# First expert's rows gathered into a slot of the weight ring, and 40 unread identity products, at a handover from mixers to experts

## The chip, the cores and the metric

One core of one Trainium2 chip runs the whole program. The metric is the device time of one execution, in microseconds. The instruction streams are PE (TensorE), DVE (VectorE), ACT (ScalarE), POOL (GpSimd) and SP (SyncE, which here only issues transfers). ACT and POOL issue transfers too.

## The reference

One layer of a hybrid encoder over 1024 tokens of width 1024, in float32:

```
h = x
h = h + hybrid_mixer(rms_norm(h, norm1_g), ...)       # mLSTM heads and gMLP groups, then @ w_out
h = h + hierarchical_moe(rms_norm(h, norm2_g), ...)
return rms_norm(h, final_g)

# hierarchical_moe, for each token: the best of 4 groups, its 2 best of 8 experts
hid = silu(xblk @ w_gate[e]) * (xblk @ w_up[e])        # 1024 -> 512
y[token] += row_w * (hid @ w_down[e])                  # 512 -> 1024
```

There are 32 experts. The weights of one are three matrices of 2 MB each, 192 MB in all.

## The kernel before, in words

The mixer runs over two halves of 512 tokens (`half_mixer`). A product of precision float32 is made of three fast products (`mm3`): each operand is split into a rounded part `r` (ACT, `ACTIVATE wr`) and a rest `l` (DVE, `TENSOR_TENSOR wl`); `split` does it for a chunk of weights, four of which can be split ahead (`SPL`).

At the end of the second half `last_out` makes the last output columns of four token tiles of 128. For each tile it adds the residual, stores it to `hd`, multiplies by norm2's gain (`scaled`, L706), transposes it (`flip`), makes the router's logits (`raw_logits`, `logits_c`), scales the rows by their norm and stores them to `xd` (`normed`, L749). Routing has five parts: `route_a` takes the maxima on DVE, `route_pr` counts the earlier tokens of each expert on PE, `route_so` and `route_c` make the places of the rows and, for the first three experts, whose numbers are fixed, the list of their tokens (`toki`, L873), and `route_d` (L885, twice for each tile) scatters a token's number and weight from POOL into the table `slots` at the places `idxs`. `ranks` then sorts the other 29 experts by their counts, with a last product on `ohp` (L913); the result, `perm`, is read by SP and POOL as the numbers of the experts whose weights and rows come next. Engines' orders inside `last_out` are written out by hand; what follows up to the second expert is ordered by the scheduler, by its own estimate of times. Later experts on PE, DVE and ACT are again in the written order.

The experts go one by one through gate, up and down (`Expert`). `fetch` gathers an expert's rows from `xd` to a tile `xe0`, `xe1` or `xe2` (L1042, an indirect transfer that POOL issues); PE transposes them (`prep`, L1102), ACT and DVE split the transposes into `xer` and `xel` (`split_ps`), and these are the operands of the gate and up products. `following` prepares the next expert's rows during the current one. The three `xe` tiles lie where the mixer's tiles lay (`stA`).

Weights come in chunks of 0.5 MB (`wchunk`), nearly all issued from SP, in the order of use. A chunk goes into the next slot of a cycle of 30: 14 of ring "early", 9 "late", 4 "ring" and 3 "tail", the last being tiles that held the mixer's transposed activations (`slot`). A load can be issued when the slot's last chunk has been split or multiplied. Loads for the first three experts are issued ahead (`prefetch`); five more go to other tiles of the activations (`prefetch_first`). In `last_out` ACT issues three chunks of the third expert's w_down into the three "tail" slots (`held`, `PD`), before the routing of the last tile. Chunks for the experts after that wait for `perm` and a free slot.

Of the kernel before, what the change touches and what calls it, by code (L numbers as in the profile page):

```python
# [15 lines left out]
AF = mybir.ActivationFunctionType  # L16
# [3 lines left out]
P = 128  # L20
T = 1024
# [4 lines left out]
TT = HALF // P  # L26
# [14 lines left out]
       [48] * 4 + [40] * 3 + [64]  # L41
SPL = 4
LOOK = 8
YS = (5, 7)
E_ = mybir.EngineType
TMS = (E_.DVE, E_.Activation)
# [10 lines left out]
TAGS = [n + str(c) for c in (2, 3, 0, 1) for n in "rl"]  # L57
MIX = "TTTSSBSSHSSBSSBSSHSSBSBSBBSBBSSS"
PF = [0, 4, 4, 5]
PD = 3  # L60
ENGS = (mybir.EngineType.SP, mybir.EngineType.Pool)
KO = [4, 5, 6, 7, 0, 1, 2, 3]
MAXX = 48
# [6 lines left out]
def trunk_kernel(ctx: ExitStack, tc: tile.TileContext, x, norm1_g, w_in, conv_qk, b_igate, b_fgate,  # L70
# [264 lines left out]
    def half_mixer(hf):  # L335
# [319 lines left out]
        for nh in range(2):  # L655
            hv = slice(nh * 512, (nh + 1) * 512)
            if last and nh:
                ws = {c: wo(c, nh) for c in CO}
                def piece(po, t, i):
                    part(po, CO[i], ws[CO[i]], t)  # L660

                with tc.manual_schedule(engines=set(MS)):
                    last_out(hf * TT, ys, piece, hv)
                with tc.issue_after(pin["POOL"].ins):
                    route_d(T // P - 2, 0)
                    route_d(T // P - 2, 1)
                    route_d(T // P - 1, 0)
                    route_d(T // P - 1, 1)
                break
            if nh:  # L670
                po = [acc() for _ in range(TT)]
                for c in CO:
                    w = wo(c, nh)
                    for t in range(TT):
                        part(po[t], c, w, t)
            elif last:
                prefetch(XO + RE + RL)
            for t in range(TT):
                nc.vector.tensor_tensor(ys[t][:, hv], po[t], ys[t][:, hv], op=OP.add)
                if last:  # L680
                    nc.sync.dma_start(hd[ds((hf * TT + t) * P, P), hv], ys[t][:, hv])
# [19 lines left out]
    def scaled(g, h, q, eng=None):  # L701
        if q == 0:
            t = g % TT
            xns[g] = yl[0][t - 1] if t else ring.tile([P, 1024], F32, name="raw")
        hv = slice(q * 512, (q + 1) * 512)
        (eng or nc.gpsimd).tensor_tensor(xns[g][:, hv], h[:, hv], g2b[:, hv], op=OP.mult)  # L706
# [26 lines left out]
    def logits(g, h):  # L733
# [4 lines left out]
        for q in range(2):  # L738
# [2 lines left out]
            nc.vector.scalar_tensor_tensor(xn, h[:, hv], rs, g2b[:, hv], op0=OP.mult, op1=OP.mult)  # L741
            nc.gpsimd.dma_start(xd[ds(g * P, P), hv], xn)

    def last_out(g0, ys, piece, hv):
        def normed(t):
            rs = logits_c(g0 + t)
            xn = xns[g0 + t]
            nc.scalar.activation(xn, xn, AF.Copy, scale=rs)
            nc.scalar.dma_start(xd[ds((g0 + t) * P, P)], xn)  # L749

        yl[0] = ys
        flip(g0, ys[0], 0)
        for t in range(TT):
            po = acc()
            piece(po, t, 0)
            if t:
                raw_logits(g0 + t - 1, 1)
                normed(t - 1)
                if t > 1:
                    route_d(g0 + t - 2, 0)  # L760
            piece(po, t, 1)
            piece(po, t, 2)
            if t:
                route_a(g0 + t - 1)
            piece(po, t, 3)
            if t:
                route_pr(g0 + t - 1)
            raw_logits(g0 + t, 0)
            nc.vector.tensor_tensor(ys[t][:, hv], po, ys[t][:, hv], op=OP.add)
            if t:  # L770
                route_so(g0 + t - 1)
            nc.scalar.dma_start(hd[ds((g0 + t) * P, P), hv], ys[t][:, hv])
            flip(g0 + t, ys[t], 1)
            scaled(g0 + t, ys[t], 0)
            if t + 1 < TT:
                if t > 1:
                    route_d(g0 + t - 2, 1)
                scaled(g0 + t, ys[t], 1)
                flip(g0 + t + 1, ys[t + 1], 0)
            if t:  # L780
                route_c(g0 + t - 1)
            if t + 1 == TT:
                prefetch_first()
            prefetch(XO + RE + RL + PF[t])
        scaled(g0 + TT - 1, ys[TT - 1], 1, nc.vector)
        raw_logits(g0 + TT - 1, 1)
        normed(TT - 1)
        prefetch(XO + RE + RL + PF[-1], eng=nc.scalar)
        for z in sources(NSTAT - 1, 2)[:PD]:
            held.append(wchunk(z, nc.scalar, True))  # L790
        route_d(g0 + TT - 3, 1)
        route_a(g0 + TT - 1)
        route_pr(g0 + TT - 1)
        route_so(g0 + TT - 1)
        route_c(g0 + TT - 1)
# [88 lines left out]
    def route_d(t, c):  # L884
        st = nc.gpsimd.indirect_dma_start(  # L885
            out=slots, out_offset=bass.IndirectOffsetOnAxis(ap=idxs[:, t, c:c + 1], axis=0),
            in_=pay[:, t, c], in_offset=None)
        for o in scat:
            tc.declare_no_dep(st.ins, o.ins, reason="every pair has a slot of its own")
        scat.append(st)  # L890
# [7 lines left out]
    def ranks():  # L898
        pc_ = sm()
        for b in range(T // P):  # L900
            nc.tensor.matmul(pc_[:MAXX, :NE], ones[:, :MAXX], masks[:, b], start=b == 0, stop=b == T // P - 1)
        for b in range(T // P):
            nc.tensor.matmul(pc_[:NE, NE:NE + 1], masks[:, b], ones[:, :1], start=b == 0, stop=b == T // P - 1)
        key = lp[0].tile([NE, NE], F32, name="key")
        nc.vector.scalar_tensor_tensor(key, pc_[:NE, :NE], float(NE), keyr, op0=OP.mult, op1=OP.add)
        kc = rt.tile([NE, 1], F32, name="kc")
        nc.vector.scalar_tensor_tensor(kc, pc_[:NE, NE:NE + 1], float(NE), keyc, op0=OP.mult, op1=OP.add)
        rk = rt.tile([NE, 1], F32, name="rk")
        nc.vector.tensor_scalar(key, key, kc, None, op0=OP.is_gt)
        nc.vector.tensor_reduce(rk, key, axis=AX.X, op=OP.add)  # L910
        oh = lp[0].tile([NE, NE], BF16, name="ohp")
        nc.vector.tensor_scalar(oh, ioe[:NE], rk, None, op0=OP.is_equal)
        nc.tensor.matmul(pc_[:1, 64:64 + NE], ecol, oh, start=True, stop=True)  # L913
        nc.vector.tensor_copy(perm, pc_[:1, 64:64 + NE])
        cnt = rt.tile([MAXX, NE], F32, name="cnt")
        nc.vector.tensor_copy(cnt, pc_[:MAXX, :NE])
        return cnt, rk
# [76 lines left out]
    def sources(e, m):  # L994
        w4 = (wg4, wu4, wd4)[m]
        z = w4[e] if isinstance(e, int) else w4[ds(e, 1)].rearrange("o p k f -> p (o k) f")
        return [z[:, 2 * c:2 * c + 2] for c in range(4)] if m < 2 else [z[:, k:k + 1] for k in range(4)]
# [20 lines left out]

    for hf in range(NHALF):
        half_mixer(hf)  # L1020
    rk = ranks()
    stA.close()
    mo = ctx.enter_context(tc.tile_pool(name="mo", bufs=2, side="right"))
    xes = [mo.tile([P, D], F32, name=f"xe{i}", bufs=1) for i in range(NXE)]
    for a in xes[NSTAT:]:
        nc.scalar.activation(a, nhalf[:, 0:1].to_broadcast([P, D]), AF.Copy)
    slots5 = slots.rearrange("(b e) w -> b e w", e=NE)
    ngat = [0]
# [1 line left out]
    def fetch(e, base, n, a=None):  # L1030
        sx_ = mo.tile([P, 1, 4], I32, name="sx_", bufs=8)
        if n <= P // 2:
            for q in range(2):
                nc.gpsimd.dma_start(sx_[q * P // 2:(q + 1) * P // 2], slots5[base:base + P // 2][:, ds(e, 1)])
        else:
            rows_ = slots5[base:base + n] if isinstance(base, int) else slots5[ds(base, n)]
            nc.gpsimd.dma_start(sx_[:n], rows_[:, ds(e, 1)])
        if a is None:
            a = xes[ngat[0] % NXE]
            ngat[0] += 1  # L1040
        at = toki[:n, e:e + 1] if isinstance(e, int) else sx_[:n, 0, 0:1]
        nc.gpsimd.indirect_dma_start(out=a[:n], out_offset=None, in_=xd,  # L1042
                                     in_offset=bass.IndirectOffsetOnAxis(ap=at, axis=0),
                                     bounds_check=T - 1, oob_is_err=False)
        return a, sx_, n

    def split_ps(ps, r, l):
        nc.scalar.activation(r, ps, AF.Copy)  # L1048
        nc.vector.tensor_tensor(l, ps, r.bitcast(F32), op=OP.subtract)

    H = P // 2
# [212 lines left out]
    for i, r in enumerate(order):  # L1264
        last = i + 1 == NE
        if i == 0:
            ahead()
            feed()
            cur = Expert(blks[r], take, pump)
            cur.prep()  # L1270
        while loads and loads[0][0] <= i + 1:
            j, e, m = loads.pop(0)
            skip[0] = (e, m) == (NE - 1, 2)
            early.extend(sources(ident_of(order[e]), m))
            if (e, m) == (NSTAT - 1, 2):
                ready.extend(held)
                del early[:len(held)]
            feed()
# [131 lines left out]
```

## Time and profile before

| | us |
|---|---|
| median of 3 runs | 1080.01 |
| lowest, highest | 1077.17, 1083.43 |
| profiled execution, its own time | 1077.55 |
| its span in the profile | 1075.8 |
| PE busy | 984.6 (92%) |
| DVE busy | 600.1 (56%) |
| ACT busy | 520.9 (48%) |
| mean granted TensorE clock | 0.968 |
| moved by DMA | 282.28 MB, mean 262 GB/s |

The profiled execution lies 2.46 us below the median of the runs, and 1.75 us of it lie outside the span. Matmuls are pipelined and their ends are modelled, so a busy PE is not PE at its peak. The mixer lasts until about 470 us; the experts run from there to about 1040 us; the rest is the final norm and the stores of the output.

### The profile page before, as it was taken

The page shows a single profiled execution, that of the slowest core. Times are in us where ns is not written, and L with a number is a line of the kernel's source. Part 1 is how long each engine was busy: PE and PEld are TensorE (multiplying, and loading weights), DVE is VectorE, ACT ScalarE, POOL GpSimd, SP SyncE. Part 2 cuts the span into 40 slices and gives each one's busy share as a digit, 9 for nine tenths or more (in the row PEclk, how much of TensorE's full clock was granted, in tenths as well). Part 3 has the DMA queues.
Part 4 walks back from the last instruction along what each step waited for, and adds up shares of the span by engine and source line. Part 5 has one row for each costly group of instructions (what it writes and reads, how often), then busy time and mean ns, then how long its engine had stood idle before and what let it go on. Part 6 is the DMA issues. An engine that isn't in the chain of part 4 may idle for free. (4 is left out here: it accounts for less than half of the span.)

```text
span 1075.8 us, 16181 instructions
## 1 busy us (share of the span) xinstructions
PE 984.6 (92%) x5489; PEld 762.7 (71%) x5489; DVE 600.1 (56%) x1234; ACT 520.9 (48%) x779; POOL 207.9 (19%) x259
## 2 busy tenths in 40 slices
PE   6999999999999999949999999999799998999960
PEld 6999887889899887737766666655566665767520
DVE  6644899656655897677834342433342455658123
ACT  6753645255534553347834433444333464758222
POOL 4310000011300000343212222321211221311123
PEclk9999999999999999979999999999899998999995
DMA  7534212444239313976999999999999999999985
GB/s 273 183 99 124 80 67 72 144 136 132 80 105 351 99 60 107 344 271 210 366 330 396 373 362 372 347 377 389 363 381 364 356 364 374 354 373 392 389 313 221
DMA packets 105460, 282.28 MB, mean 262 GB/s; under 512 B 13666, under 2 KB 40370, under 8 KB 105376
## 3 DMA queue, kind: packets, MB, share of 16 engines
q1 hardware_dynamic: 92080, 251.76, 63.8%
q0 software_dynamic: 11712, 24.75, 8.9%
q10 hardware_dynamic: 1584, 4.72, 1.2%
q8 instruction: 44, 0.72, 0.3%
q14 instruction: 40, 0.33, 0.1%
HBM read 261.62 MB, written 25.72 MB: 267 GB/s over the span
## 5 line engine op out<-in xcount | busy, mean ns | idle before, releaser
L107 DVE TENSOR_TENSOR wl<-raw,wr 128x1024 fp32r<-128x1024 f32 (+2 forms) x219 | 259.1, 1191 | 195.8 <-ACT wr L106 183.1
L106 ACT ACTIVATE wr<-raw 128x1024 fp32r<-128x1024 f32 (+2 forms) x219 | 223.6, 1028 | 229.7 <-PE acc L113 166.4
L111 PE MATMUL acc<-wr,r 128*128 128x512 f32 (+2 forms) x688 | 265.1, 386 | 1.7 <-ACT r L1048 0.9
L112 PE MATMUL acc<-wl,r 128*128 128x512 f32 (+2 forms) x688 | 260.5, 379 | 0.0
L113 PE MATMUL acc<-wr,l 128*128 128x512 f32 (+2 forms) x560 | 208.3, 375 | 0.0
L111 PEld LDWEIGHTS acc<-wr,r 128*128 128x128 f32 x688 | 130.5, 190 | 25.5 <-issue 5.1
L112 PEld LDWEIGHTS acc<-wl,r 128*128 128x128 f32 x688 | 130.8, 190 | 15.2 <-issue 0.5
L1056 PE MATMUL acc<-raw,r 128*64 128x256 f32 (+1 forms) x864 | 132.3, 453 | 2.6 <-ACT r L1083 2.4
L113 PEld LDWEIGHTS acc<-wr,l 128*128 128x128 f32 x560 | 106.2, 190 | 11.4 <-DVE l L235 0.6
L1056 PEld LDWEIGHTS acc<-raw,r 128*64 128x64 f32 x864 | 59.8, 138 | 58.8 <-issue 27.9
L111 PE MATMUL acc<-wr,xer 128*128 128x512 f32 x144 | 59.9, 416 | 0.0
L113 PE MATMUL acc<-wr,xel 128*128 128x512 f32 x144 | 57.4, 398 | 0.0
L112 PE MATMUL acc<-wl,xer 128*128 128x512 f32 x144 | 57.3, 398 | 0.0
L1102 PEld LDWEIGHTS sm<-ident,xe 64*128 64x128 f32 (+1 forms) x272 | 33.9, 197 | 31.8 <-issue 15.8
L1056 PE MATMUL acc<-raw,xer 128*64 128x256 f32 x448 | 52.9, 383 | 0.7 <-ACT xer L1083 0.7
L1102 PE MATMUL sm<-ident,xe 64*128 64x64 f32 (+1 forms) x272 | 38.8, 286 | 14.9 <-DMA xe<-xd,toki 8.6
L111 PE MATMUL acc<-r,wr 128*128 128x512 f32 x128 | 51.5, 402 | 0.0
L112 PE MATMUL acc<-l,wr 128*128 128x512 f32 x128 | 51.0, 398 | 0.0
L113 PE MATMUL acc<-wr,r 128*128 128x512 f32 x128 | 50.7, 396 | 0.0
L113 PE MATMUL acc<-r,wl 128*128 128x512 f32 x128 | 50.5, 395 | 0.0
L1056 PEld LDWEIGHTS acc<-raw,xer 128*64 128x64 f32 x448 | 30.8, 137 | 17.3 <-issue 1.0
L1083 ACT ACTIVATE r<-sm 128x256 f32<-128x256 f32 (+1 forms) x28 | 12.7, 453 | 44.4 <-PE sm L1153 44.1
(477 smaller groups left out, 1368.9 us busy)
## 6 DMA issues: line engine op xcount, KB each, us to landing
raw<-in_w_up_dram SPq DMA_DIRECT2D x119, 512.0 KB, 11.6
raw<-in_w_down_dram SPq DMA_DIRECT2D x113, 512.0 KB, 11.2
raw<-in_w_gate_dram SPq DMA_DIRECT2D x111, 512.0 KB, 11.6
raw<-in_w_in_dram SPq DMA_DIRECT2D x24, 412.0 KB, 3.5
raw<-in_w_in_dram SPq DMA_DIRECT2D x16, 512.0 KB, 3.9
raw<-in_w_out_dram SPq DMA_DIRECT2D x16, 512.0 KB, 3.6
raw<-in_w_in_dram SPq DMA_DIRECT2D x16, 410.0 KB, 4.0
l<-in_w_gate_dram SPq DMA_DIRECT2D x11, 512.0 KB, 12.8
```

Of the source, the lines that this page charges most:

```text
L106: nc.scalar.activation(r[:, :n], raw[:, :n], AF.Copy)
L107: nc.vector.tensor_tensor(l[:, :n], raw[:, :n], r[:, :n].bitcast(F32), op=OP.subtract)
L111: nc.tensor.matmul(ps, ar, br, start=first, stop=False)
L112: nc.tensor.matmul(ps, ar, bl, start=False, stop=False)
L113: nc.tensor.matmul(ps, al, br, start=False, stop=last)
L1056: nc.tensor.matmul(ps[q * H:(q + 1) * H, :n], x, w[:, q * n:(q + 1) * n], start=first, stop=last)
L1083: nc.scalar.activation(x, ps[0][:, :kt * H], AF.Copy)
L1102: nc.tensor.transpose(ps[-1][:, k % per * w:(k % per + 1) * w], xk_[:w, k], ident[:w, :w])
```

## The change

The gather of expert 0's rows goes to a slot of the weight cycle (the first "tail" slot) and is issued ahead of the last tile's two slot stores, which were issued before the gathers in the source. The second and third expert's gathers then follow as before, to `xe0` and `xe1`; `xe2` is first used by an expert with up to 64 rows and is filled once with a finite value on ACT. `PD` falls to 2, since one slot is taken, and the two chunks of w_down that are left are issued from ACT behind the split of expert 0's transposes. The other two come from SP. `busy(n)` transposes the identity n times into a PSUM bank that nobody reads: 16 times ahead of the last tile's routing, 24 times behind `ranks`. The last half-row multiply of `scaled` goes from DVE to POOL.

```diff
+WARM = (16, 24)
-PD = 3
+PD = 2
...
-                    route_d(T // P - 1, 0)
-                    route_d(T // P - 1, 1)
...
+    def busy(n):
+        ps = acc()
+        for i in range(n):
+            nc.tensor.transpose(ps[:, 0:P], ident, ident)
...
-        scaled(g0 + TT - 1, ys[TT - 1], 1, nc.vector)
+        scaled(g0 + TT - 1, ys[TT - 1], 1)
         raw_logits(g0 + TT - 1, 1)
         normed(TT - 1)
         prefetch(XO + RE + RL + PF[-1], eng=nc.scalar)
-        for z in sources(NSTAT - 1, 2)[:PD]:
-            held.append(wchunk(z, nc.scalar, True))
         route_d(g0 + TT - 3, 1)
+        busy(WARM[0])
         route_a(g0 + TT - 1)
...
-        nc.tensor.matmul(pc_[:1, 64:64 + NE], ecol, oh, start=True, stop=True)
+        pin["RK"] = nc.tensor.matmul(pc_[:1, 64:64 + NE], ecol, oh, start=True, stop=True)
...
         half_mixer(hf)
+    rows0 = slot()
+    pin["XG"] = nc.gpsimd.indirect_dma_start(out=rows0, out_offset=None, in_=xd,
+                                             in_offset=bass.IndirectOffsetOnAxis(ap=toki[:, 0:1], axis=0),
+                                             bounds_check=T - 1, oob_is_err=False)
+    with tc.issue_after(pin["XG"].ins):
+        route_d(T // P - 1, 0)
+        route_d(T // P - 1, 1)
     rk = ranks()
     stA.close()
+    with tc.issue_after(pin["RK"].ins):
+        busy(WARM[1])
...
-    for a in xes[NSTAT:]:
+    for a in xes[NSTAT - 1:]:
         nc.scalar.activation(a, nhalf[:, 0:1].to_broadcast([P, D]), AF.Copy)
...
+        if isinstance(e, int) and e == 0:
+            return rows0, sx_, n
...
-        nc.scalar.activation(r, ps, AF.Copy)
+        pin["XE"] = nc.scalar.activation(r, ps, AF.Copy)
...
             cur.prep()
+            with tc.issue_after(pin["XE"].ins):
+                for z in sources(NSTAT - 1, 2)[:PD]:
+                    held.append(wchunk(z, nc.scalar))
```

The scheduler moves more than the diff says. PE, from the last product of `ranks` on, before (`xe_4921` are the rows of expert 0; three rows of products with `xer` and `xel` make one precise product):

```order
L913 MATMUL sm<-ohp,ecol 1x32
L1102 MATMUL sm<-ident,xe_4921 128x128 x8
L111 MATMUL acc<-wr,xer 128x512
L112 MATMUL acc<-wl,xer 128x512
L113 MATMUL acc<-wr,xel 128x512
L111 MATMUL acc<-wr,xer 128x512
```

and now (`l_4895` is the ring slot with the rows of expert 0, `xe_4961` holds those of expert 1):

```order
L916 MATMUL sm<-ohp,ecol 1x32
L746 MATMUL acc<-ident 128x128 x24
L1116 MATMUL sm<-ident,l_4895 128x128 x8
L112 MATMUL acc<-wr,xer 128x512
L113 MATMUL acc<-wl,xer 128x512
L1116 MATMUL sm<-ident,xe_4961 128x128 x3
L114 MATMUL acc<-wr,xel 128x512
```

Three transposes of expert 1's rows have moved from behind the 24 gate products of expert 0 to behind the second of them; the other five stand behind the 24th.

POOL, from the last norm on, before:

```order
L119 TENSOR_TENSOR rs_4809<-ms_4807,nhalf 128x1
L885 DMA slots<-pay,idxs 36864x4 x3
L1042 DMA xe_4921<-xd,toki 128x1024
L1042 DMA xe_4922<-xd,toki 128x1024
L1187 TENSOR_LOAD perm
L885 DMA slots<-pay,idxs 36864x4 x2
L1042 DMA xe_4923<-xd,toki 128x1024
```

and now:

```order
L120 TENSOR_TENSOR rs_4809<-ms_4807,nhalf 128x1
L888 DMA slots<-pay,idxs 36864x4 x3
L1025 DMA l_4895<-xd,toki 128x1024
L888 DMA slots<-pay,idxs 36864x4 x2
L1056 DMA xe_4961<-xd,toki 128x1024
L1056 DMA xe_4962<-xd,toki 128x1024
```

The scheduler had already put two gathers ahead of the last two slot stores; now there is one, and the second expert's gather stands behind them.

DVE, behind `toki`, now:

```order
L913 TENSOR_REDUCE rk<-key 32x1
L108 TENSOR_TENSOR wl<-raw,wr 128x1024
L885 SCALAR_TENSOR_TENSOR idxs<-pos,e_4846 128x2
L915 TENSOR_SCALAR ohp<-row_304,rk 32x32
L108 TENSOR_TENSOR wl<-raw,wr 128x1024
L917 CAST perm<-sm 1x32
```

Before, `ohp` and `perm` stood ahead of the first of these splits, and `idxs` behind it; now the first split stands ahead of `ohp`, and the second ahead of `perm`.

## Rows read from the trace of the kernel before

**Rows 1.** Busy time by stages of 20 us: us of each engine with its number of instructions, then the granted TensorE clock as a share of full speed, the DMA share and GB/s.

```profile
480.00:500.00 20.00, 15.59 (x68) 12.93 (x69) 11.26 (x12) 11.32 (x14) 12.41 (x16) 0.79 0.61 217
...
500.00:520.00 20.00, 18.94 (x88) 15.22 (x87) 17.76 (x18) 16.34 (x19) 3.84 (x5) 1.00 0.86 290
...
560.00:580.00 20.00, 20.00 (x112) 12.78 (x109) 9.36 (x10) 10.94 (x17) 7.51 (x8) 1.00 1.03 397
```

**Rows 2.** What SP's queue (the weight loads) waited for from 560 to 580 us, the first of its rows: us in total, times, the longest.

```profile
SPq L989 <- DMA raw<-in_w_up_dram: 5.4, 4, 2.0
```

**Rows 3.** The same from 545 to 560 us.

```profile
SPq L989 <- PE acc L1056: 8.7, 7, 6.4
```

**Rows 4.** Busy time by stages of 1 us at the handover (columns as in the first group).

```profile
471.00:472.00 1.00, 0.00 (x0) 0.00 (x0) 0.86 (x6) 0.00 (x0) 0.88 (x1) 0.64 0.52 188
...
488.00:489.00 1.00, 1.00 (x5) 0.77 (x5) 0.00 (x0) 0.10 (x1) 0.00 (x0) 0.82 1.05 417
```

**Rows 5.** PE's timeline at the handover: start, us, instruction, in brackets the idle time before it and what ended it.

```profile
468.18 0.34 PE L850 MATMUL sm<-masks,ones 128*128 128x32 bf16 x7
...
472.40 0.19 PE L851 MATMUL sm<-masks,su 128*128 128x32 bf16 x1 [3.88 <-DVE masks L838]
...
475.62 0.18 PE L913 MATMUL sm<-ohp,ecol 32*1 32x32 bf16 x1 [1.06 <-DVE ohp L912]
...
484.42 1.94 PE L1102 MATMUL sm<-ident,xe 128*128 128x128 f32 x8 [8.61 <-DMA xe<-xd,toki]
...
488.70 0.40 PE L111 MATMUL acc<-wr,xer 128*128 128x512 f32 x1
...
492.60 0.40 PE L113 MATMUL acc<-wr,xel 128*128 128x512 f32 x1
...
492.83 1.04 PE L1102 MATMUL sm<-ident,xe 128*128 128x128 f32 x8
...
493.63 0.48 PE L111 MATMUL acc<-wr,xer 128*128 128x512 f32 x1
```

**Rows 6.** POOL's timeline there, in the same columns.

```profile
461.90 1.31 POOL L706 TENSOR_TENSOR y<-y,g2b 128x512 f32<-128x512 f32 x1
...
469.03 0.57 POOL L119 TENSOR_TENSOR rs<-ms,nhalf 128x1 f32<-128x1 f32 x1 [5.82 <-DVE ms L117]
...
477.01 2.08 POOL L1042 DMA_INDIRECT xe<-xd,toki  x1 [3.66 <-ACT wr L106]
...
479.39 2.00 POOL L1042 DMA_INDIRECT xe<-xd,toki  x1 [0.30 <-DVE wl L107]
...
481.70 1.01 POOL L885 DMA_INDIRECT slots<-pay,idxs  x1 [0.31 <-DVE wl L107]
...
484.30 1.04 POOL L1042 DMA_INDIRECT xe<-xd,toki  x1 [0.30 <-issue]
```

**Rows 7.** DMA issues, each from a stretch that holds this one alone: the last store to `xd` (at 470.8), the gathers issued at 477.01, 479.39 and 484.30 (128 rows each, 0.5 MB), and one of 64 rows at 498.44. The last number is the time from issue to landing in us.

```profile
xd<-y ACTq DMA_DIRECT2D x1, 512.0 KB, 3.7
...
xe<-xd,toki POOLq DMA_INDIRECT x1, 7.1
...
xe<-xd,toki POOLq DMA_INDIRECT x1, 10.0
...
xe<-xd,toki POOLq DMA_INDIRECT x1, 6.9
...
xe<-xd,sx__5187 POOLq DMA_INDIRECT x1, 4.3
```

**Rows 8.** DVE's timeline at the handover.

```profile
468.54 0.15 DVE L728 TENSOR_TENSOR ssq<-sq 128x1 f32<-128x1 f32 x1
...
474.46 0.16 DVE L873 TENSOR_TENSOR toki<-tokc,sm 128x3 int32<-128x3 f32 x1 [1.06 <-PE sm L871]
...
475.35 0.22 DVE L912 TENSOR_SCALAR ohp<-row,rk 32x32 bf16<-32x32 bf16 x1
...
476.04 0.14 DVE L875 SCALAR_TENSOR_TENSOR ws<-d,sg 128x1 f32<-128x1 f32 x1
...
478.08 0.15 DVE L882 SCALAR_TENSOR_TENSOR idxs<-pos,e 128x2 int32<-128x2 f32 x1
...
478.15 3.49 DVE L107 TENSOR_TENSOR wl<-raw,wr 128x1024 fp32r<-128x1024 f32 x3
```

**Rows 9.** ACT's timeline there.

```profile
467.78 0.19 ACT L724 ACTIVATION_READ_ACCUMULATOR acc<-y 128x1 f32 x1
...
470.81 0.33 ACTq L749 DMA_DIRECT2D xd<-y  x1
...
473.67 0.30 ACT L843 ACTIVATE eg<-lga,ng 128x4 f32<-128x4 f32 x1 [2.89 <-DMA xd<-y]
...
485.59 0.60 ACT L1048 ACTIVATE xer<-sm 128x512 fp32r<-128x512 f32 x1 [7.66 <-issue]
```

**Rows 10.** Busy time by stages of 1 us at a second place where PE stood idle for 5.75 us, until 772.99 (columns as in the first group).

```profile
767.00:768.00 1.00, 0.24 (x3) 0.05 (x1) 0.96 (x2) 0.72 (x2) 0.93 (x1) 1.00 1.04 418
...
771.00:772.00 1.00, 0.00 (x0) 0.00 (x0) 0.73 (x2) 0.98 (x3) 0.41 (x1) 0.83 1.01 393
...
778.00:779.00 1.00, 1.00 (x4) 0.78 (x4) 0.00 (x0) 0.01 (x1) 0.00 (x0) 0.76 1.04 328
```

**Rows 11.** SP's timeline from 470 to 500 us, its first row: the gate weights of the fourth expert, four loads.

```profile
478.19 3.81 SPq L989 DMA_DIRECT2D raw<-in_w_gate_dram  x4
```

## The prediction

> **What bounds the kernel now.** I read three views in this order: the busy time by stages, the waits of SP's queue, then engine by engine the 40 us in which the mixer hands over to the experts.
>
> From 560 us on the transfers set the pace: a stage of 20 us shows a DMA share of 1.03 [rows 1], and what SP's next weight load waits for is an earlier load [rows 2]. Just before, from 545 to 560 us, it is the reverse: SP waits 8.7 us for products of PE, which must free a slot of the ring [rows 3]. So the loads are tied to PE's progress until about 556 us, and after that the remaining bytes flow at a fixed rate. A microsecond that PE gains at the first expert is therefore a microsecond at the end, as long as the loads before 556 us keep up.
>
> At the handover PE is nearly idle for 16 us. Its last product of the mixer stage starts at 468.18; then it waits 3.88 us for the masks and 8.61 us for the gathered rows of expert 0, whose transposes begin at 484.42 [rows 5]. The granted clock shows this too: 0.64 in the slice from 471 to 472 us means a fall from full (2.4 GHz) to half (1.2 GHz) at 471.3, some 2.8 us after PE's last work; 0.82 from 488 to 489 means full again at 488.4, some 3.9 us after PE resumed [rows 4]. The up products of expert 0 start at 493.63 [rows 5]. That is my mark: whatever moves it moves the end.
>
> The wait of 8.61 us is read backwards on POOL [rows 6]. The gather of expert 0's rows is issued at 477.01 and lands 7.1 us later [rows 7], at 484.1. Its inputs were there earlier: the token list (`toki`) at 474.6 [rows 8], and the last store to `xd` at 474.5, 3.7 us after its issue at 470.81 [rows 7, 9]. What it still waited for, by the program, was the memory of `xe0`, which it shares with tiles of the mixer stage; their last reader is the product on `ohp`, at 475.62 [rows 5].
>
> **The change, part by part.**
>
> *The multiply moved from DVE to POOL.* On DVE the sum of squares waits behind it until 468.54 [rows 8]; ACT had that sum ready at 467.97 [rows 9]. So 0.57 us are gained in the routing chain. POOL pays 1.3 us for it in a gap of 5.82 us [rows 6]: nothing.
>
> *Three w_down loads taken from ACT's queue.* They delayed the exponentials, and the splits behind them, to 473.67 [rows 9]. Now ACT splits sooner, but DVE's half of a split waits for the routing chain (below), so this gains nothing by itself.
>
> *16 products after the last logits.* At full clock a transpose of this size takes 0.10 us (8 between 492.83 and 493.63) [rows 5], so 1.6 us in a gap of 3.88: nothing on the path. They may keep the clock up for the routing's small products; DVE waits 1.06 us for these before `toki` [rows 8]. I count nothing for it, with about 0.7 us as the bound.
>
> *The rows of expert 0 gathered into a ring slot.* The slot is free when PE has left the mixer, so only `toki` (now about 473.9) and the `xd` store (about 473.9) hold it. I put its start at 474.2 to 475.4, the latter if the 1.2 us between the product on `ohp` and the old gather [rows 5, 6] come again. Landing after 4.3 to 7.1 us [rows 7], it is there at 478.5 to 482.5, against 484.1.
>
> *24 products before the transposes.* The product on `ohp` now stands behind a split of 1.2 us on DVE (three in 3.49 [rows 8]) and behind `idxs` (477.0, below), at 477.3 instead of 475.62. The 24 then take 2.4 us at full clock; at half, at 0.24 each (8 in 1.94 from 484.42) [rows 5], they would take 5.8. I take half at the start, since the clock fell 2.8 us after PE's last work here and 4.4 us after it in a second place, and full again 3.9 to 5.5 us later, as in the two recoveries [rows 4, 10]: PE is free at 482.0 to 482.9, eight transposes and two products later at about 484.8. The 24 hide partly behind the landing rows; what shows is hidden behind the next item, and if that cover goes they cost up to 2 us.
>
> *The second gather.* This decides. The order of the changed program puts three transposes of expert 1's rows after only two products of expert 0's gate; before, all 24 gate products came first. PE works in order, so gate 0 now waits for the second gather. And that is issued no earlier: on POOL the two last slot stores stand ahead of it. They need `idxs`, which came 3.62 us after `toki` [rows 8]; 0.69 of these (from `ohp` to `ws`) now fall behind the split, so `idxs` starts at 473.9 + 2.9 = 476.8, and the first store at 477.2. Two stores at 1.3 each with their gap [rows 6] put the second gather at 479.8, against 479.39. It took 10.0 us there; the other two took 7.1 and 6.9 [rows 7]. I take 7.1, because the first gather of before met what this one will meet: a slow POOL part of 2 us, as DVE splits at the same time (1.04 without) [rows 6, 8], and gate loads of the fourth expert that start about 1 us after it [rows 11]. These loads wait for `perm`, which now stands behind two splits, so they come at about 479 to 481 instead of 478.19 to 482. Landing: 486.9. The bounds are 4.3 (64 rows with little else under way) and 10.0.
>
> *PE after it.* From 487.2 remain 3 + 5 transposes at 0.10 and 22 products at 0.229 (17 between 488.70 and 492.60) [rows 5], together 5.8 us, at full clock: PE has then been at work since 477.3 and idle for 2.4. The up products start at 493.0 instead of 493.63: **0.6 us gained**.
>
> *Loads moved later.* 1.5 MB that arrived by 480 us now come after PE's first transposes, about 4 us of transfer at the 397 GB/s of a full stage. From 480 to 520 us the share is 0.61 and 0.86, so 10 us are free [rows 1]. One slot less for one turn of the ring makes each load wait one chunk longer (six products, 1.4 us); the ring holds 30 chunks, some 40 us of PE's work, so PE does not see it, and from the second turn on the depth is the old one. The fill of a third `xe` buffer costs ACT one pass of about 1.1 us in the 7.7 us in which it waits [rows 9]. All this I count at nothing.
>
> **Sum.** The profiled execution took 1077.55 us; minus 0.6 gives 1076.95. It lies 2.46 below the median of the three runs, so I forecast 1080.01 − 0.6 = **1079.4 us**.
>
> **The rivals.**
>
> *Nothing blocks the second time.* If the second gather lands after 4.3 us, at 484.1, PE hardly waits: its two products are done at about 484.8 or a little sooner, then 0.3 and 5.8 us at most, so up at 490.2 to 490.6; I write 490.2: 3.4 us gained, 1076.6. With the clock held through the routing and the 24 products done by 479.9, the rows' own landing binds and it is 4.6: 1075.4. For it speaks that the three w_down loads no longer run just before; against it that 7.1, 10.0 and 6.9 are all that this place has shown [rows 7].
>
> The Trainium skill, "DMA: Bandwidth & Descriptors", section "Anatomy of one DMA", gives such a transfer about 2 us plus its bytes at 436 GB/s, an estimate of 3.2 us for 0.5 MB; by it the second gather lands at 483.0 and the time would be near 1076.6. The trace does not agree: its three gathers of this size took twice that or more.
>
> *The second gather is the new wait, and long.* If it takes the 10.0 us of its predecessor, it lands at 489.8. PE has then stood idle for about 5 us since its two first products, longer than the 2.8 and 4.4 us after which the clock was seen to fall [rows 4, 10], and runs the next 3.9 to 5.5 us (the two recoveries seen) at half, which loses 2.0 to 2.8. Up starts at 490.1 + 5.8 + 2.4 = 498.3, **4.7 us late: 1084.7**; without the fall 2.3 late, 1082.3. It decides from a landing after 487.5 on (493.63 − 5.8 − 0.3), only 0.6 behind my figure. For it speaks that all four gate loads now start within 2 us of it, and that the loads on ACT follow at about 484; against it, that before it stood behind the first gather's 0.5 MB and now does not.
>
> The Trainium skill, same page, section "Issuing engines are not separate DMA queues", says that transfers started by different engines interleave on the same 16 DMA engines, so taking loads out of the way of one gather and into that of the next speaks against this change. The trace agrees: with gate loads under way the same gather took 6.9 to 10.0 us, where 64 rows with little else under way took 4.3 [rows 7, 11].
>
> *The change doesn't do what it says.* If the first gather is held as long as before, by the `xd` store or by POOL, its rows come at about 484 with the second gather right behind, and the times are equal: 1080.0.
>
> **How the numbers follow.** Chances: forecast (within 1.5 us of it) 0.50, no second wait 0.22, long second wait 0.20, no earlier first gather 0.08. Forecast and rivals span 1075.4 to 1084.7; the scatter of a median of runs (three span 1077.17 to 1083.43) widens each case by about 1.5. A range of **1075.5 to 1084.0** then leaves out less than half of the late rival with a fallen clock and of the best case, together under 2 in 10. 0.5%, about what a measurement of this kernel can tell from no change, is 5.4 us. None of the cases reaches it by itself; with the scatter of a median of runs the best case does now and then, and so does the late one with a fallen clock: faster 0.08, within 0.86, slower 0.06.
>
> **What would show it.** Right: the transposes of the ring slot start at 480 to 483; after two products of gate 0 PE waits 1.5 to 4 us for expert 1's rows; up starts near 493; the second gather is issued at 479 to 480. The clock is back at full before 484. Wrong: no wait after the two products (the first rival), a wait of over 4 us with a clock at half behind it (the second), or transposes that start at 484 again. A shift at the end that differs by more than 2 us from the shift at up 0 would refute the premise that PE's progress is handed on one to one.

## The result and the profile after

Before: 1079.09 us, the median of 11 runs (1076.02 to 1083.43). After: 1085.78 us, the median of 11 runs (1083.81 to 1090.65). The ratio is 1.0072, with an interval of 1.0058 to 1.0086: the change makes the kernel slower by 6.7 us between the medians (6.3 to 9.3 by the interval). I had forecast 1079.4 and a range up to 1084.0. The profiled execution of after has a span of 1086.2 us and a time of 1088.02, 2.2 above its median.

Executions of the same code reach the handover at different times. In this document's 14 profiles the mixer's last four transposes start between 463.7 and 467.8 us. I call that start M and count from it: M is 465.94 in the profile of before and 467.58 in the one of after.

PE in the profile after, from M on (start, us, instruction, idle time before it and what ended it), to be read against [rows 5]:

```profile
467.58 0.64 PE L718 MATMUL acc<-ident,y 128*128 128x128 f32 x4
...
470.10 1.95 PE L746 MATMUL acc<-ident 128*128 128x128 f32 x16
...
478.94 4.74 PE L746 MATMUL acc<-ident 128*128 128x128 f32 x24
483.52 1.06 PE L1116 MATMUL sm<-ident,l 128*128 128x128 f32 x8
...
493.14 0.88 PE L1116 MATMUL sm<-ident,xe 128*128 128x128 f32 x3 [7.58 <-DMA xe<-xd,toki]
...
500.61 0.48 PE L112 MATMUL acc<-wr,xer 128*128 128x512 f32 x1
```

The rows of expert 0 are there in time: the transposes of the slot start at M + 15.94, where before they started at M + 18.48. Two gate products follow, and then PE waits 7.58 us for expert 1's rows. The up products start at 500.61, that is M + 33.03 against M + 27.69: 5.3 us late.

POOL, DVE, ACT and SP at that place, for [rows 6, 8, 9, 11]:

```profile
467.62 1.26 POOL L705 TENSOR_TENSOR y<-y,g2b 128x512 f32<-128x512 f32 x1 [2.77 <-DVE skey L860]
...
474.36 0.96 POOL L888 DMA_INDIRECT slots<-pay,idxs  x1 [0.30 <-issue]
476.67 1.06 POOL L1025 DMA_INDIRECT l<-xd,toki  x1 [1.35 <-DVE kc L910]
478.91 4.36 POOL L888 DMA_INDIRECT slots<-pay,idxs  x1 [1.18 <-DVE ohp L915]
483.57 0.96 POOL L888 DMA_INDIRECT slots<-pay,idxs  x1 [0.31 <-issue]
484.84 1.04 POOL L1056 DMA_INDIRECT xe<-xd,toki  x1 [0.31 <-issue]
```
```profile
467.48 1.61 DVE L865 TENSOR_SCALAR so<-row,skey 128x128 bf16<-128x128 bf16 x3
...
474.78 0.58 DVE L865 TENSOR_SCALAR so<-row,skey 128x128 bf16<-128x128 bf16 x3
...
476.24 0.16 DVE L876 TENSOR_TENSOR toki<-tokc,sm 128x3 int32<-128x3 f32 x1 [0.88 <-PE sm L874]
...
477.36 1.20 DVE L108 TENSOR_TENSOR wl<-raw,wr 128x1024 fp32r<-128x1024 f32 x1
478.49 0.14 DVE L885 SCALAR_TENSOR_TENSOR idxs<-pos,e 128x2 int32<-128x2 f32 x1
...
478.70 1.21 DVE L108 TENSOR_TENSOR wl<-raw,wr 128x1024 fp32r<-128x1024 f32 x1
...
480.03 2.34 DVE L108 TENSOR_TENSOR wl<-raw,wr 128x1024 fp32r<-128x1024 f32 x2
```
```profile
484.62 0.37 ACTq L992 DMA_DIRECT2D r<-in_w_down_dram  x1
...
485.02 0.45 ACTq L992 DMA_DIRECT2D l<-in_w_down_dram  x1
```
```profile
480.77 2.45 SPq L992 DMA_DIRECT2D raw<-in_w_gate_dram  x4
```

The first of the last two slot stores takes POOL 4.36 us; the one at 474.36 took 0.96. So the second gather is issued at 484.84. By then SP has issued four loads of 0.5 MB and ACT is issuing two more; their data go ahead of the gather's or along with them. PE starts on its rows 8.3 us after its issue.

Stages of after, the third of them against [rows 1], and two of before in the same columns:

```profile
488.00:493.00 5.00, 0.00 (x0) 0.00 (x0) 0.00 (x0) 0.00 (x0) 1.74 (x4) 0.67 1.02 411
493.00:495.00 2.00, 1.86 (x6) 1.70 (x7) 0.00 (x0) 0.00 (x0) 1.58 (x3) 0.50 0.37 131
500.00:520.00 20.00, 18.83 (x89) 14.97 (x88) 17.41 (x17) 16.07 (x19) 3.74 (x6) 1.00 0.55 187
505.00:510.00 5.00, 4.38 (x18) 2.95 (x17) 4.85 (x6) 4.67 (x6) 0.45 (x1) 1.00 0.10 14
```
```profile
488.00:493.00 5.00, 5.00 (x23) 4.07 (x23) 2.70 (x3) 3.18 (x3) 2.41 (x5) 0.96 0.54 194
505.00:510.00 5.00, 5.00 (x23) 4.05 (x22) 4.28 (x5) 3.65 (x4) 0.00 (x0) 1.00 0.91 315
```

PE is empty from 488 to 493 us, and the clock is at half (0.50) when it resumes. The transfers pay later: from 505 to 510 us the DMA share is 0.10 where it was 0.91, and from 500 to 520 us 0.55 where it was 0.86. What holds them is the ring, which a waiting PE doesn't empty. This is the view of SP's waits from 476 to 520 us; the longest was 9.0 us before:

```profile
SPq L992 <- DVE wl L108: 30.6, 9, 14.9
```

In the 55 us after M, SP's queue (q1) and ACT's (q10) moved 9.64 MB, and 11.64 before. That is the view of the DMA queues for these 55 us (packets, MB, share of 16 engines), after and before:

```profile
q1 hardware_dynamic: 2112, 7.69, 40.1%
...
q10 hardware_dynamic: 618, 1.95, 9.1%
```
```profile
q1 hardware_dynamic: 2511, 9.13, 48.1%
...
q10 hardware_dynamic: 768, 2.51, 12.6%
```

From 560 to 580 us the transfers run without a break in both kernels (a DMA share of 1.02 in after, 1.03 before [rows 1]). The 2.0 MB that are missing take 5.4 us at the 370 GB/s of the stage from 700 to 800 us; PE's own delay at up 0, 5.3 us, is as large.

### The profile page after: what moved, and what is told of

Its sections match the earlier page's. It is cut to its first block, busy times and chain, and to the rows that moved or that the text cites. A ratio compares the mean times of both kernels' runs of the same rounds, so it can differ in the third digit from the quotient of the medians.

```text
span 1086.2 us, 16269 instructions
## 1 busy us (share of the span) xinstructions
PE 994.7 (92%) x5529; PEld 770.7 (71%) x5529; DVE 599.6 (55%) x1233; ACT 521.4 (48%) x780; POOL 206.8 (19%) x260
## 5 line engine op out<-in xcount | busy, mean ns | idle before, releaser
L1070 PE MATMUL acc<-raw,r 128*64 128x256 f32 (+1 forms) x848 | 129.8, 453 | 1.3 <-ACT r L1097 1.0
L1070 PE MATMUL acc<-raw,xer 128*64 128x256 f32 x480 | 57.6, 388 | 0.7 <-ACT xer L1097 0.7
L1070 PEld LDWEIGHTS acc<-raw,xer 128*64 128x64 f32 x480 | 33.2, 139 | 19.1 <-issue 2.7
L1167 PE MATMUL sm<-ident,hid 128*128 128x128 f32 x100 | 18.3, 297 | 19.4 <-DVE hid L1160 19.4
```

Source lines behind the costliest of these rows:

```text
L1070: nc.tensor.matmul(ps[q * H:(q + 1) * H, :n], x, w[:, q * n:(q + 1) * n], start=first, stop=last)
L1167: nc.tensor.transpose(ps[:, j * P:(j + 1) * P], self.hid[b][:, j * P:(j + 1) * P], ident)
```

## The experiments

Theory: PE stands behind expert 1's rows, whose gather is issued late behind a slow slot store. Rival 1: the w_down loads moved later, and the slot taken from the ring, are the cost themselves. Rival 2: the multiply on POOL and the 40 products delay the handover. Medians are of 6 or 12 runs (11 in the first two rows). Each later run's ratio is to runs of before of the same session, with medians of 1078.44 to 1078.56, so ratios compare better than medians. "Up 0 ends" is the start of the 24th up product of expert 0; MB are those of q1 and q10 in the 55 us after M.

| run | median us | ratio to before, interval | expert 1's transposes, M + | up 0 ends, M + | MB |
|---|---|---|---|---|---|
| before | 1079.09 | | 26.89 | 33.05 | 11.64 |
| after | 1085.78 | 1.0072, 1.0058 to 1.0086 | 25.56 | 38.39 | 9.64 |
| e1 | 1078.88 | 1.0004, 0.9993 to 1.0016 | 25.89 | 34.91 | 10.95 |
| e2 | 1086.47 | 1.0074, 1.0058 to 1.0091 | 25.18 | 38.73 | 9.68 |
| e3 | 1083.47 | 1.0045, 1.0028 to 1.0061 | 27.55 | 35.43 | 10.80 |
| e4 | 1077.98 | 0.9996, 0.9985 to 1.0007 | 17.77 | 29.08 | 12.01 |
| f1 | 1077.79 | 0.9998, 0.9986 to 1.0009 | 17.85 | 29.16 | 11.84 |
| f2 | 1087.07 | 1.0082, 1.0066 to 1.0098 | 24.13 | 37.68 | 8.99 |
| f3 | 1086.73 | 1.0085, 1.0070 to 1.0099 | 22.15 | 35.04 | 9.55 |
| f4 | 1085.49 | 1.0073, 1.0056 to 1.0090 | 25.59 | 38.29 | 9.91 |
| h1 | 1077.56 | 0.9998, 0.9982 to 1.0013 | 16.74 | 28.25 | 12.16 |
| h2 | 1077.64 | 0.9998, 0.9984 to 1.0012 | 18.08 | 29.40 | 11.73 |
| h3 | 1077.74 | 0.9998, 0.9986 to 1.0011 | 21.68 | 30.38 | 12.21 |
| h4 | 1078.92 | 1.0011, 0.9996 to 1.0025 | 18.29 | 31.71 | 11.18 |

### e1: PE's order as before

```diff
...
             ex = Expert(blks[order[i + 1]], take, pump)
-            ex.prep()
+            with ExitStack() as st:
+                if i == 0:
+                    st.enter_context(tc.issue_after(pin["G0"].ins))
+                ex.prep()
```

`pin["G0"]` is the last gate product of expert 0.

> The changed kernel, with expert 1's transposes held behind the last of the 24 gate products of expert 0, as they stood before. Theory (PE, in order, stands behind expert 1's rows after two gate products): the wait of 7.6 us shrinks to under 3 us, gate 0 ends near 490.5, up 0 starts near 494 instead of 500.6, time 1078.5 to 1080.5. Rival 1 (the loads moved later and the slot lost to the rows cost the time): up 0 comes sooner all the same, but the end stays at 1084 or more. Rival 2 (the multiply on POOL and the 40 products delay the handover): 1084 or more, too.

PE, around the wait:

```profile
492.04 1.97 PE L1116 MATMUL sm<-ident,xe 128*128 128x128 f32 x8 [2.78 <-DMA xe<-xd,toki]
```

The wait shrinks to 2.78 us and the loss is gone. The gather is as late as in after (M + 17.3 in both); it is PE's order that made it cost. Both rivals fall as the main cause, since everything of theirs is still in.

### e2: the gather ahead of the slot stores

```diff
-    with tc.issue_after(pin["XG"].ins):
-        route_d(T // P - 1, 0)
-        route_d(T // P - 1, 1)
...
+    pin["X1"] = nc.gpsimd.indirect_dma_start(out=xes[0], out_offset=None, in_=xd,
+                                             in_offset=bass.IndirectOffsetOnAxis(ap=toki[:, 1:2], axis=0),
+                                             bounds_check=T - 1, oob_is_err=False)
+    with tc.issue_after(pin["X1"].ins):
+        route_d(T // P - 1, 0)
+        route_d(T // P - 1, 1)
...
```

> The changed kernel, with expert 1's gather issued ahead of the last two slot stores; PE's order with transposes of expert 1 after two gate products stays. Theory (that gather is late because it stands behind slow slot stores): it is issued at 479 to 480.5 instead of 484.84 and lands at 487 to 489, PE waits 2 to 4 us instead of 7.6, the clock stays full, up 0 starts at 493 to 495.5, time 1078.5 to 1081. Rival 1 (loads moved, slot lost): 1084 or more. Rival 2 (multiply on POOL, products): 1084 or more.

POOL, DVE and PE:

```profile
479.70 3.40 POOL L1036 DMA_INDIRECT xe<-xd,toki  x1 [0.37 <-issue]
```
```profile
479.86 2.34 DVE L108 TENSOR_TENSOR wl<-raw,wr 128x1024 fp32r<-128x1024 f32 x2
```
```profile
492.60 0.67 PE L1121 MATMUL sm<-ident,xe 128*128 128x128 f32 x2 [8.10 <-DMA r<-in_w_down_dram]
```

A miss. The gather starts 5 us sooner, but now it is the gather that takes 3.40 us on POOL beside DVE's splits, until 483.10, and SP's four loads (issued from 480.60 on) are ahead of its data. PE starts on its rows at 492.60, that is M + 25.18, hardly sooner than in after (M + 25.56). The row names a w_down load as what ended the wait; the gather's own last completion is in the trace at 492.19, 12.5 us after its issue. So the late issue isn't all: what has been issued ahead of its data counts too.

### e3: without the 40 products

```diff
-WARM = (16, 24)
+WARM = (0, 0)
...
```

> The changed kernel without its 40 identity products. Theory: the 24 only stand ahead of products that wait for expert 1's rows anyway, so PE waits longer and up 0 comes when it did, time 1085 to 1087 (up to 1 us worse if the clock is lower at the resume). Rival 2 (the products delay the handover by their 4.7 us): 1081 to 1083.

1083.47 us is between the two. The scheduler put all gate products of expert 0 ahead of expert 1's transposes here, as in e1, so the run changes two things. Against e1, which has the products and this order, it is 4.6 us slower by the medians, while up 0 ends only 0.5 us later from M. By the profiles the two are closer: from M to the end of the span 613.9 us in e3 and 613.0 in e1 (609.9 before, 618.6 in after). So the handover explains little of e3's median, and the rest stays open.

### e4: the w_down loads early on ACT

```diff
         prefetch(XO + RE + RL + PF[-1], eng=nc.scalar)
+        for z in sources(NSTAT - 1, 2)[:PD]:
+            held.append(wchunk(z, nc.scalar, True))
...
-            with tc.issue_after(pin["XE"].ins):
-                for z in sources(NSTAT - 1, 2)[:PD]:
-                    held.append(wchunk(z, nc.scalar))
```

> The changed kernel, with its two w_down loads issued on ACT before the routing of the last tile, as before, and not behind PE's first transposes. Theory: PE still waits for expert 1's rows, 1083.5 to 1086. Rival 1 (the loads moved later cost the time): 1079 to 1081.

The time is rival 1's, but the trace shows another cause: with ACT's queue longer, the scheduler set the splits later and POOL's gathers first.

```profile
479.06 1.01 POOL L1058 DMA_INDIRECT xe<-xd,toki  x1 [0.30 <-ACT xe L1040]
```
```profile
485.58 0.71 PE L1118 MATMUL sm<-ident,xe 128*128 128x128 f32 x4 [0.69 <-DMA xe<-xd,toki]
```

Expert 1's rows are there at 485.58, and PE waits 0.69 us. f4 takes the two apart.

### f1: the splits held until the second gather is issued

```diff
...
+            with tc.issue_after(g.ins):
+                nc.gpsimd.memset(zz[:, 0:1], 0.0)
+            pin["ZZ"] = nc.vector.tensor_copy(zz[:, 1:2], zz[:, 0:1])
...
-                st.enter_context(tc.issue_after(pin["TOK"].ins))
+                st.enter_context(tc.issue_after(pin["ZZ"].ins))
```

`g` is expert 1's gather, `zz` a small tile of its own; the block that now starts behind `pin["ZZ"]` holds the splits for expert 0's gate.

> The changed kernel, with VectorE's part of the weight splits held until the second gather has been issued (a one-column fill on POOL behind that gather, read by a copy on DVE ahead of the splits). Theory A (the slot store takes 4.36 us because DVE's splits run beside it): both stores take about 1.0 us, the second gather is issued at 480 to 481 instead of 484.84. If late issue alone made it late, it lands at 487 to 488.5; theory B (it lands when the engines have carried what was issued ahead of it, above all the four gate loads of the fourth expert) says 488.5 to 491, since these loads come sooner, too. PE's wait 2.5 to 5.5 us, time 1079.5 to 1083. If A is wrong, the store still takes over 3 us and the time stays at 1085 to 1087.

POOL, DVE, PE and SP:

```profile
478.67 1.02 POOL L888 DMA_INDIRECT slots<-pay,idxs  x1 [0.30 <-issue]
479.99 0.96 POOL L888 DMA_INDIRECT slots<-pay,idxs  x1 [0.31 <-issue]
481.26 1.04 POOL L1056 DMA_INDIRECT xe<-xd,toki  x1 [0.30 <-issue]
...
482.60 2.01 POOL L1056 DMA_INDIRECT xe<-xd,toki  x1 [0.19 <-issue]
```
```profile
482.52 1.22 DVE L108 TENSOR_TENSOR wl<-raw,wr 128x1024 fp32r<-128x1024 f32 x1
```
```profile
485.39 0.49 PE L1121 MATMUL sm<-ident,xe 128*128 128x128 f32 x2 [0.62 <-DMA xe<-xd,toki]
```
```profile
483.76 5.38 SPq L992 DMA_DIRECT2D raw<-in_w_gate_dram  x4
```

Theory A holds: the stores take 1.02 and 0.96 us, the second gather is out at 481.26 and lands 4.1 us later, faster than I expected, as SP's loads come only behind it. The whole loss is gone, with all other parts of the change in place. The third gather, at 482.60, runs beside a split and takes 2.01.

### f2 and f3: less ahead of the second gather

f2 issues the two w_down loads behind expert 0's SiLU. f3 also holds the four gate loads until the gather is issued:

```diff
...
+            pre.extend(slot() for _ in range(PD + 1))
+            with tc.issue_after(g.ins):
+                nc.gpsimd.memset(pre[PD][:, 0:1], 0.0)
...
```

> The changed kernel, with its two w_down loads issued on ACT behind the SiLU of expert 0 and not behind PE's first transposes, so 1 MB less stands ahead of the second gather; all issue times up to there stay. Theory B: it lands 1.5 to 3 us sooner, at 490 to 491.6, up 0 starts at 497.5 to 499, time 1083 to 1084.5. Rival (late issue alone): it lands at 493 as before, 1085 to 1087.

> As the run with the w_down loads behind the SiLU, and the four gate loads of the fourth expert held as well until the second gather has been issued (their first slot is filled in one column on POOL behind that gather). Theory B: nothing of these 3 MB stands ahead of the gather; issued at about 484.8 as before, it lands at 488.5 to 490.5, PE's wait 3 to 5 us instead of 7.6, up 0 at 495.5 to 497.5; the loads themselves lose about 4 us of the queue, so the end comes at 1080.5 to 1084. Rival (late issue alone): landing at 492 to 493.5 and 1086 or more.

In f3, PE and SP:

```profile
485.87 0.71 PE L1120 MATMUL sm<-ident,xe 128*128 128x128 f32 x3 [4.02 <-DMA xe<-xd,toki]
...
502.33 0.50 PE L113 MATMUL acc<-wl,r 128*128 128x512 f32 x1 [2.94 <-DVE wl L108]
```
```profile
482.17 2.46 SPq L992 DMA_DIRECT2D raw<-in_w_gate_dram  x4
```

The landing moves as theory B says: from M + 25.56 to 24.13 with 1 MB less ahead and to 22.15 with 3 MB less, PE's wait from 7.58 to 6.09 and 4.02. But the time doesn't follow; both runs are as slow as after, with 8.99 and 9.55 MB. One reason stands right behind up 0. In both runs DVE now does the multiply that makes `hid` ahead of four weight splits, which come first in after; it waits 3.8 us for PE's product, and PE then waits 2.94 us (2.95 in f2) for a split behind it. DVE in f3, then in after:

```profile
499.26 0.69 DVE L1164 TENSOR_TENSOR hid<-hid,acc 128x512 f32<-128x512 f32 x1 [3.81 <-PE acc L114]
...
501.07 1.21 DVE L108 TENSOR_TENSOR wl<-l,wr 128x1024 fp32r<-128x1024 f32 x1
```
```profile
505.26 1.23 DVE L108 TENSOR_TENSOR wl<-l,wr 128x1024 fp32r<-128x1024 f32 x1
...
509.81 0.68 DVE L1160 TENSOR_TENSOR hid<-hid,acc 128x512 f32<-128x512 f32 x1
```

So the two runs change two things, and what the late loads cost by themselves isn't shown. The pair e1 and f3 shows what it does: up 0 ends at M + 34.91 and 35.04, and the times lie 8 us apart, with 10.95 MB against 9.55. But at PE's transposes of a later expert's `hid`, which come 226.40 us after M in before, e1 is 1.02 us late by then and f3 5.46 (before, e1, f3; M is 466.15 and 463.72 in the last two):

```profile
692.34 0.65 PE L1153 MATMUL sm<-ident,hid 128*128 128x128 f32 x4 [1.13 <-DVE hid L1146]
```
```profile
693.57 0.66 PE L1167 MATMUL sm<-ident,hid 128*128 128x128 f32 x4 [1.13 <-DVE hid L1160]
```
```profile
695.58 0.66 PE L1171 MATMUL sm<-ident,hid 128*128 128x128 f32 x4 [1.13 <-DVE hid L1164]
```

### f4: the w_down loads early, on SP

As e4, with `nc.sync` for `nc.scalar`; the orders on PE, POOL and DVE at the handover are those of after.

> The changed kernel, with its two w_down loads issued early as before the change, but on SP's queue, so that the orders on PE, DVE, POOL and the splits on ACT stay as the change made them. Theory B: they are out of the second gather's way as in the run that issues them late: landing 490 to 491.6, up 0 at 497.5 to 499, and 1 MB is there sooner, but PE sets the end: 1082.5 to 1084.5. Rival 1 (the loads moved later are the cost themselves): 1078.5 to 1080 whatever PE's wait is.

1085.49 us, where rival 1 had 1078.5 to 1080. The lead of the early loads (3.54 MB within 15 us of M, 2.23 in after) has shrunk to 0.2 MB at M + 35; I take it that the ring is full behind a waiting PE either way. Theory B's 1082.5 to 1084.5 is missed, too: the loads came in the way of the last `xd` store (6.3 us to its landing, 2.9 in after), and expert 0's rows were late instead; PE waited 6.74 us for these. So f4 is no clean test of rival 1. The pair f1 and h1 below is: the loads are late in f1 and early in h1, and neither has the loss.

### h1 to h4: what is left once the loss is gone

h1 is f1 with the w_down loads early on ACT, h2 is f1 with the multiply back on DVE, h3 is the kernel before with the splits held, h4 is f1 without the 40 products.

> The changed kernel with the splits held behind the second gather, and its two w_down loads issued early on ACT as before the change. Premise of the prediction (a shift at up 0 is handed on one to one): expert 0's up products end about 3 us sooner than before the change, counted from the mixer's last transposes, so 1075 to 1076. Theory C (only the weights brought in count, and an earlier PE gains what the ring then takes more): 0.5 to 1 MB more by 95 us after these transposes, 1076 to 1078.5, no more than 2.5 us under the kernel before.

> The changed kernel with the splits held, and the moved multiply back on DVE. Prediction's step (on DVE it delays the sum of squares by 0.57 us): the stretch from the mixer's last transposes to the token list grows from 8.7 to about 9.3 us. Other reading (on POOL it makes the DVE work beside it slower by as much): 8.5 to 8.8 us either way. Time 1077 to 1079 by both.

> The kernel before, with nothing of the change, but VectorE's splits held behind its second gather. Theory A (a DMA instruction on POOL makes no headway while a split runs on DVE): the first two gathers take 1.0 us on POOL instead of 2.08 and 2.00, the first lands about 1 us sooner; up products 0 to 1.5 us sooner; time 1077 to 1079, no measurable difference, since the weights set the end. If the holding of the splits is itself what helped the changed kernel: 1076 or less.

> The changed kernel with the splits held, without its 40 identity products. The transposes of the slot start when its rows land, about 1 us sooner, but at half clock (1.94 us for eight instead of 1.05), and the first 3 to 5 us of products at half clock too: expert 0's up products end 0.5 to 2.5 us later than with the products; time 1077.5 to 1080. Rival (the products cost their time): 1 us sooner and 1077 or less.

POOL of h3, its first two gathers; DVE's token list in h2 (M is 465.61 there):

```profile
477.97 1.06 POOL L1042 DMA_INDIRECT xe<-xd,toki  x1 [3.68 <-DMA l<-in_w_down_dram]
...
481.93 1.05 POOL L1042 DMA_INDIRECT xe<-xd,toki  x1 [0.30 <-issue]
```
```profile
473.94 0.16 DVE L876 TENSOR_TENSOR toki<-tokc,sm 128x3 int32<-128x3 f32 x1 [0.88 <-PE sm L874]
```

In h3 both gathers take 1.05 us where they took 2.08 and 2.00 [rows 6], and up 0 ends 2.7 us sooner from M, more than expected. In h2 the token list comes at M + 8.33; with the multiply on POOL it came at M + 8.74 (f1) and 8.66 (after). Without the 16 products it comes at 8.87 with the multiply on POOL (e3, h4) and at 8.52 and 8.54 with it on DVE (before, h3). So the multiply on POOL costs 0.3 to 0.4 us, the 16 products bring 0.1 to 0.2, and both readings that I had written down were off. In h4 up 0 ends 2.55 us later than in f1 and the median is 1.1 us higher, inside the intervals: the products save PE's clock, but no time that these runs can show. h1's 1077.56 lies in theory C's range and above the premise's 1075 to 1076. None of the four, nor f1, beats the kernel before: with up 0 ending 1.3 to 4.8 us sooner, the ratio stays at 0.9998 to 1.0011.

## Why the prediction was wrong

**The step that failed is the second gather's issue.** I named it as the step that decides and priced the two slot stores ahead of it at 1.3 us each with their gap, from rows with no split beside them. From M the second gather was issued at 17.26 instead of the 13.86 that 479.8 means there, and 3.35 of these 3.4 us are the store, 4.36 where the row had 1.01. The row that should have warned me was in my own text: two gathers with a slow POOL part of 2 us "as DVE splits at the same time". I used it for the landing and not for the stores, although the order of the changed program set DVE's splits right beside them. f1 shows it by removal, h3 without the change.

**Its rows** reached PE 8.3 us after the issue, where I had 7.1 for the landing and 0.3 from there to PE: SP's four loads and ACT's two had been issued ahead of it or with it. f2 and f3 show this with 1 MB and 3 MB taken away. In e2 the gather was started early, and these loads still got ahead of its data.

**PE behind it.** The order (two gate products, three transposes) was read rightly, and e1 shows that it is what turns a late gather into a late PE. The clock at half for the first products behind the wait cost the rest: 7.47 us from expert 1's first transposes to up 0, where I had 5.8 at full clock. Added up: 3.4 + 0.9 + 1.7 is 6.0, which is up 0 at M + 33.03 instead of 27.06. This is the mechanism of my second rival (the long second wait), with chance 0.20 and 1084.7 us; its gather was late by another cause.

**The rows of expert 0** came as forecast: issued at 476.67, landed after 4.5 us, transposes not waiting for them. **The 24 products** took 4.74 us (2.4 to 5.8 forecast), the 16 took 1.95 inside PE's gap. **The multiply on POOL** was booked as a gain of 0.57 us; it is a loss of 0.3 to 0.4, since DVE's three `so` took 1.61 us beside it and 0.58 otherwise. **The moved loads** were counted at nothing: right for the moving as such (f1 and h1).

**The premise**, that a shift of PE at up 0 is handed on one to one, held roughly for the run it was made for (5.3 us at up 0, 6.7 between the medians, 6.3 to 9.3 by the interval) and is wrong as a rule: on the early side 1.3 to 4.8 us at up 0 gave nothing measurable. The profiles show how far it holds. Counted from M, PE's shift against before stays the same to 0.1 us from M + 55 to M + 238 in each of the other 13 profiles, although the transfers run without a break from about 560 us (M + 94) on: 5.7 us late in after, 5.5 in f3 and 1.0 in e1, and 3.9, 3.1 and 2.4 us early in h1, f1 and h3. At PE's last expert product the same runs are 9.2, 11.9 and 1.7 us late, and 0.7 to 0.8 early. So a shift is handed on for 180 us, and what becomes of it, the loss of the lead above all, is decided behind that.

The weights in by M + 55 order the runs: the five with less than 10 MB are slower by 0.7% or more, all with 10.95 or more lie within 0.2%, and e3, with 10.80, is between. PE's shift at M + 55 orders them as well (5.5 us or more in the five, 1.5 or less in all others), and since a load waits for PE to free its slot, no run separates the two causes. What stays open is the size: 1 MB is 2.7 us at 370 GB/s, and by their ratios the five lost 1.7 to 3.5 us more than that; and how the lead of f1, h1 and h3 (24.8 to 25.3 MB in 95 us from M, 24.0 before) is lost behind M + 238.

## What to carry to other kernels

Before you price an instruction that is moved, look at what will run beside it in the new order, above all on the engine that it shares a path with; a duration read from a quiet place is a lower bound. Where an engine works in order, a single early instruction that waits for a late transfer can cost more than the change gains: hold such work back behind the products that are ready. And read an engine's place well behind the mark, too: in f3 the mark came where e1 has it, and a changed order right behind it kept PE waiting for 3 us.

## What the hardware showed that I had not expected

**An indirect transfer that POOL starts while DVE splits weights is held until a split ends** (subtractions of 128x1024 with both inputs in SBUF). Alone it takes 0.96 to 1.06 us on POOL; beside splits 2.0 to 2.1 (before, f1, h3), 3.3 to 3.5 (e2, f2, f3, f4) and 4.36 (after, e1, e3). It ends 0.87 to 0.93 us behind the end of a split: in after at 483.27, with the last split's end at 482.37; in e2 at 483.10, with 482.20. Here it matters which of the two starts first: in after the gather that starts at 476.67 takes 1.06 us, though a split starts beside it at 477.36, and the store at 478.91, 0.21 us into a split, takes 4.36. Starts that lie closer together went either way: f4's gather at 478.50, 0.07 us ahead of a split, took 3.34, and e4's at 479.06, 0.04 us behind a split's start, took 1.01. ACT's half of a split doesn't do this: in f1 the store at 478.67 takes 1.02 us beside one. Which of several splits in a row lets the transfer through isn't shown. Plain transfers without an index list took 0.62 instead of 0.58 us beside f1's splits. The Trainium skill, "SBUF — State Buffer", section "SBUF: two separate sides", says that GpSimd and VectorE share one pair of ports under an exclusive lock, which the one that starts first has for its whole instruction, and in "Who interferes with whom" that a VectorE instruction with two inputs in SBUF contends with a GpSimd instruction that reads SBUF, and not with one that only writes it. The trace agrees in kind, by these numbers, if POOL reads the index list in SBUF for an indirect transfer, which no run here shows.

**The same in the other direction:** three DVE comparisons that take 0.58 us together took 1.61 beside a POOL multiply of 1.26 us, in after and the ten other runs that have it there.

**The rows of a gather of 0.5 MB** reached PE 4.1 us after its issue with little ahead of it (f1), 8.3 with six loads ahead or along with it (after) and 12.9 in e2, where its own POOL part was held while four loads were being issued.
